# Expert tiles of a two-layer mixture-of-experts kernel: one transpose block on TensorE, the activation product ahead of the weight copies on VectorE, and empty scatter rows left out

## The chip, the cores and the metric

The kernel runs on one core of a Trainium2 chip. The metric is the device time of one launch in microseconds (us). A core has TensorE (PE in the rows; its weight loads have their own lines, PEld), VectorE (DVE), ScalarE (ACT), GpSimd (POOL) and SyncE (SP), each with its own instruction stream in program order, and 16 DMA engines that all queues share. SPq, POOLq and ACTq are the instructions of those engines that start a DMA.

## The reference

Two layers work on 256 latent tokens and 256 context tokens with 1024 channels. Each layer is a token mixer (state space, gated MLP, differential attention) followed by a mixture of experts: 64 experts of hidden width 256, eight of them chosen for each token, and one shared expert. The change touches the routed experts only:

```python
def swiglu(x, wg, wu, wd):
    return (jax.nn.silu(x @ wg) * (x @ wu)) @ wd

def routed_experts(h, eidx, w, w_gate, w_up, w_down):
    ...   # sort the (token, expert) pairs by expert, pad each expert's list to whole blocks
    def block_ffn(args):
        tok, wt, e = args
        return swiglu(h_pad[tok], w_gate[e], w_up[e], w_down[e]) * wt[:, None]
    yb = lax.map(block_ffn, (row_tok.reshape(n_blk, MOE_BLOCK), row_w.reshape(n_blk, MOE_BLOCK), blk_e))
    return jax.ops.segment_sum(yb.reshape(n_rows, d), row_tok, num_segments=t + 1)[:t]
```

Layer 0 routes 512 tokens (4096 pairs), layer 1 only the 256 latent ones (2048 pairs).

## The kernel before

Everything is float32. In each layer the mixer is followed by `route` (which tokens go to which unit of which expert), `experts` and `combine`.

**Units and tiles.** A unit is up to 64 tokens of one expert, a tile is two units (lanes) side by side on the 128 rows. The number of tiles follows from the data: 43 in layer 0 and 25 in layer 1, 68 in all. Rows of a unit that no token fills are empty. Tables in memory, made by `route`, say for each tile which token a row gathers (`t_gather`, an empty row's index lies out of bounds) and which row of `acc` it adds to (`t_scatter`, an empty row goes to one of 64 spare rows behind each lane's n rows).

**Weights.** A unit needs its expert's gate, up and down matrices, 3 MB in all. `load` (three DMAs from SP's queue) brings them into one of four slots of a ring `raw`; two tiles fill the ring. If the slot already holds that expert, the DMAs are skipped by a condition. From the slot DVE copies them on: gate and up in four pieces b = 0 to 3 for each lane (`copy_gu`, tiles `gu`, single-buffered across tiles), down in one piece for each lane (`copies_dn`, tiles `dn`, double-buffered). DVE waits for a unit's load with a semaphore that SP raises, and needs a register load (`TENSOR_LOAD`) for the slot's address and the count to wait for. When a lane's down copy is done the slot is free, and SP issues the load of the unit four further on; SP raises the signal for an earlier load only when it has issued later ones.

**A tile on TensorE.** `gate_up(t)` is 32 matmuls of 64-column weights, two at a time for the two lanes (`tile_position`), into `pg`. `x_t(t+1)` transposes the next tile's gathered rows, eight 128x128 transposes into `px`. `down(t-1)` is 16 matmuls of 64-column weights into `py`. `h_t(t-1)` transposes the activation `sg` of the earlier tile, two 128x128 transposes into `ph`. ACT does silu, the copies of `px` to `xt` and `ph` to `ht`, and scales `py` to `y`; DVE multiplies silu by up (`act`, L1580) and makes the weights of the rows (L1569); POOL issues the gather of three tiles ahead and the scatter of `y`, an indirect DMA that adds into `acc`.

**What sets the order.** `experts` is written under a manual schedule: each engine runs its instructions as the Python code emits them. `body(t)` emits h_t(t-1), gate_up(t), the gate/up copies of pieces 0 to 2 of tile t+1 (each lane after its own register load and wait), act(t), the copies of piece 3, x_t(t+1), the gather, down(t-1), and the down copies of tile t+1 with SP's loads. Tiles whose number depends on the data run under nested `If`s (`rest`); the last branch emits h_t and down of the last tile.

Of the kernel before, what the change touches and what calls it, by code (L numbers as in the profile page):

```python
# [11 lines left out]
F32 = mybir.dt.float32  # L12
# [3 lines left out]
ALU = mybir.AluOpType  # L16
AX = mybir.AxisListType
ET = mybir.EngineType
# [3 lines left out]
P = 128  # L22
D = 1024
# [4 lines left out]
T = NLAT + NCTX  # L28
# [32 lines left out]
def shape_consts():  # L61
# [7 lines left out]
    for n in (T, NLAT):  # L69
        pm, ln = p % UNIT, p // UNIT  # L70
        cols += [1 + n + pm, ln * (n + UNIT) + n + pm]
    for t in range(NT):
# [28 lines left out]
class Build:  # L101
# [1108 lines left out]
    def load(self, l, raw, eid, cond, slot_off):  # L1210
# [4 lines left out]
        for j, nm in enumerate(("w_exp_gate", "w_exp_up", "w_exp_down")):  # L1215
            w = self.A[nm][l][ds(e, 1)]
            src = w.rearrange("o (p k) n -> p (o k) n", p=P) if j < 2 else w.rearrange("o (k p) n -> p (o k) n", p=P)
            o = 2048 * j
# [22 lines left out]
    def route(self, l, n, rt, fD, acc, tab, raw, pool, pp):  # L1241
# [14 lines left out]
        nc.gpsimd.memset(zt, 0.0)  # L1256
        r0, r1 = n, LANES * (n + UNIT)
        while r0 < r1:
            m = min(P, r1 - r0)
            nc.scalar.dma_start(acc[r0:r0 + m, :], zt[:m])  # L1260
            r0 += m
        M = pool.tile([P, nt, NE], F32, name="M")
# [213 lines left out]
        pcc = self.C("pcol")  # L1476
        k1 = 1 if n == T else 3
        v = pool.tile([P, nx], F32, name="lv")
# [5 lines left out]
        V.tensor_copy(tb["gather"], g)  # L1484
        V.tensor_scalar(g, v, 0.5, None, op0=ALU.is_gt)
        V.tensor_scalar(g, g, pcc[:, k1:k1 + 1], -1.0, op0=ALU.mult, op1=ALU.mult)
        V.tensor_scalar(g, g, pcc[:, k1 + 1:k1 + 2], None, op0=ALU.add)
        V.tensor_add(g, g, v)
        tb["scatter"] = tab.tile([P, nx], I32, name="t_scatter")
# [3 lines left out]
    def experts(self, l, n, tb, fD, acc, raw):  # L1493
# [9 lines left out]
        with tc.tile_pool(name="ex", bufs=1, reuse_waits="tile") as pool, \  # L1503
# [5 lines left out]
            SG = [pool.tile([P, EH], F32, name="sg%d" % i) for i in range(2)]  # L1509
            HT = pool.tile([P, 2, P], F32, name="ht")  # L1510
            Y = [pool.tile([P, D], F32, name="y%d" % i) for i in range(2)]
# [16 lines left out]
            def copies_gu(t):  # L1528

                srcs = []  # L1530
                for ln in range(LANES):
                    u = t * LANES + ln
                    off, wv = regs(tb["unit"][0:1, 0:2, u], ET.DVE)
                    off = nc.s_assert_within(off, 0, (SLOTS - 1) * EW, skip_runtime_bounds_check_because=why)
                    V.wait_ge(s_ld, wv)
                    src = raw[:, ds(off, EW)]
                    srcs.append(src)
                    for b in range(3):
                        copy_gu(ln, b, src)
                return srcs  # L1540
# [41 lines left out]
            def h_t(t):  # L1582
                for k in range(2):
                    nc.tensor.transpose(pH[:, k * P:(k + 1) * P], SG[t % 2][:, k * P:(k + 1) * P], ident)
                nc.scalar.copy(HT.rearrange("p a b -> p (a b)"), pH[:, 0:256])  # L1585

            def down(t):
                for hf in range(2):
                    for k in range(2):
                        for ln in range(LANES):  # L1590
                            r = slice(UNIT * ln, UNIT * ln + UNIT)
                            nc.tensor.matmul(pY[hf][r, :], HT[:, k, r], DN[ln][t % 2][:, k, 512 * hf:512 * hf + 512],  # L1592
                                             start=(k == 0), stop=(k == 1), tile_position=(0, UNIT * ln))
                    nc.scalar.activation(Y[t % 2][:, 512 * hf:512 * hf + 512], pY[hf], AF.Copy, scale=W[t % 4])  # L1594
                nc.gpsimd.indirect_dma_start(out=acc, out_offset=bass.IndirectOffsetOnAxis(ap=tb["scatter"][:, t:t + 1], axis=0),  # L1595
                                             in_=Y[t % 2], in_offset=None, compute_op=ALU.add)

            def body(t):
                if t > 0:
                    h_t(t - 1)  # L1600
                gate_up(t)
                if t + 1 < tmax:
                    srcs = copies_gu(t + 1)
                act(t)
                if t + 1 < tmax:
                    for ln in range(LANES):
                        copy_gu(ln, 3, srcs[ln])
                    x_t(t + 1)
                if t + AHEAD < tmax:
                    gather(t + AHEAD)  # L1610
                if t > 0:
                    down(t - 1)
                if t + 1 < tmax:
                    copies_dn(t + 1, srcs)

            def rest(t):

                if t < tmax:
# [3 lines left out]
                    with more.Else():  # L1622
                        h_t(t - 1)
                        down(t - 1)
                else:
                    h_t(t - 1)
                    down(t - 1)
            for t in range(AHEAD):
                gather(t)
            srcs = copies_gu(0)  # L1630
            for ln in range(LANES):
                copy_gu(ln, 3, srcs[ln])
            copies_dn(0, srcs)
# [49 lines left out]
    def whole(self):  # L1683
# [8 lines left out]
        for l in range(DEPTH):  # L1692
# [3 lines left out]
            fD = self.dram.tile([n, D + NE], F32, name="f_%d" % l)  # L1696
            acc = self.dram.tile([LANES * (n + UNIT), D], F32, name="acc%d" % l)
            f = rows(fD, n // P)
# [37 lines left out]
```

## Time and profile before

| | |
|---|---|
| three runs | 2009.74, 2008.34 and 2000.35 us, median 2008.34 |
| the profiled execution | 2000.67 us, span 1998.8 us |
| mean granted TensorE clock | 0.941 |
| PE busy | 1792.3 us, 90% of the span |
| DVE, ACT, POOL busy | 1176.3, 595.6, 528.3 us |
| moved by DMA | 440.11 MB, 220 GB/s on the mean |
| expert tiles, layer 0 | about 634 to 1180 us, 43 tiles |
| expert tiles, layer 1 | about 1618 to 1966 us, 25 tiles |

A row of a timeline gives the start in us, the length in us, engine, line and operation, then what it writes and reads, how many like it follow one another, and in brackets how long the engine stood idle before and what released it. A row of the windows gives, for a stretch of time, the busy time of each engine with its number of instructions, then the granted clock, the share of time in which the DMA engines were busy, and the rate. A row of waits gives engine, line, what it waited for, the sum, the number and the longest.

### The profile page before, as it was taken

The page shows a single profiled execution, that of the slowest core. Times are in us where ns is not written, and L with a number is a line of the kernel's source. Part 1 is how long each engine was busy: PE and PEld are TensorE (multiplying, and loading weights), DVE is VectorE, ACT ScalarE, POOL GpSimd, SP SyncE. Part 2 cuts the span into 40 slices and gives each one's busy share as a digit, 9 for nine tenths or more (in the row PEclk, how much of TensorE's full clock was granted, in tenths as well). Part 3 has the DMA queues.
Part 4 walks back from the last instruction along what each step waited for, and adds up shares of the span by engine and source line. Part 5 has one row for each costly group of instructions (what it writes and reads, how often), then busy time and mean ns, then how long its engine had stood idle before and what let it go on. Part 6 is the DMA issues. An engine that isn't in the chain of part 4 may idle for free. (4 is left out here: it accounts for less than half of the span.)

```text
span 1998.8 us, 30455 instructions
## 1 busy us (share of the span) xinstructions
PE 1792.3 (90%) x10137; PEld 1040.6 (52%) x10137; DVE 1176.3 (59%) x2346; ACT 595.6 (30%) x1139; POOL 528.3 (26%) x407
## 2 busy tenths in 40 slices
PE   5798999999998999999998974989989689998894
PEld 2686876778765333333333323767789443333331
DVE  7687554333666666666665637823563666646563
ACT  3343343332222222222222215423453212221211
POOL 4354301222311222222222224321143012232221
PEclk8898999999999999999999976979999799999986
DMA  8113524453778677787898957346544379999974
GB/s 276 49 44 115 176 95 140 150 193 130 269 248 314 198 214 210 228 292 232 301 323 293 381 168 263 119 156 214 194 145 169 142 299 309 317 304 388 377 259 116
DMA packets 168310, 440.11 MB, mean 220 GB/s; under 512 B 26261, under 2 KB 82995, under 8 KB 151226
## 3 DMA queue, kind: packets, MB, share of 16 engines
q1 hardware_dynamic: 132044, 340.89, 46.6%
q0 software_dynamic: 20448, 62.41, 13.7%
q10 hardware_dynamic: 15630, 34.56, 4.8%
q8 instruction: 86, 1.41, 0.3%
q14 instruction: 102, 0.84, 0.1%
HBM read 658.36 MB, written 58.17 MB: 358 GB/s over the span
## 5 line engine op out<-in xcount | busy, mean ns | idle before, releaser
L1575 PE MATMUL pg<-gu,xt 128*64 128x512 f32 x2176 | 497.4, 610 | 1.5 <-ACT xt L1567 1.5
L1544 DVE COPY gu<-raw 128x1024 f32 x560 | 364.1, 694 | 207.8 <-SPq L1237 97.0
L1575 PEld LDWEIGHTS pg<-gu,xt 128*64 128x64 f32 x2176 | 153.8, 140 | 298.0 <-issue 283.7
L1595 POOL DMA_INDIRECT acc<-y,t_scatter x68 | 124.3, 1828 | 606.6 <-ACT ht L1585 430.0
L1592 PE MATMUL py<-dn,ht 128*64 128x512 f32 x1088 | 251.3, 604 | 5.4 <-ACT ht L1585 5.4
L1550 DVE COPY dn<-raw 128x2048 f32 x140 | 172.0, 1229 | 120.0 <-PE py L1592 100.5
L135 PE MATMUL mm<-uh,whi 128*128 128x512 f32 (+1 forms) x544 | 198.6, 365 | 6.8 <-ACT rx L848 4.6
L137 PE MATMUL mm<-uh,wlo 128*128 128x512 f32 (+1 forms) x544 | 194.9, 359 | 0.5 <-DVE wlo L314 0.5
L136 PE MATMUL mm<-ul,whi 128*128 128x512 f32 (+1 forms) x544 | 193.7, 356 | 0.0
L314 DVE TENSOR_TENSOR wlo<-raw,whi 128x1024 fp32r<-128x1024 f32 x77 | 97.8, 1271 | 114.1 <-ACT whi L311 113.9
L1579 ACT ACTIVATE sg<-pg 128x256 f32<-128x256 f32 x68 | 26.1, 384 | 452.1 <-PE pg L1575 452.1
L1524 POOL DMA_INDIRECT xg<-f,t_gather x74 | 101.0, 1365 | 180.8 <-DMA acc<-sh_y 56.2
L1592 PEld LDWEIGHTS py<-dn,ht 128*64 128x64 f32 x1088 | 72.8, 138 | 132.5 <-issue 118.7
L1594 ACT ACTIVATE y<-py,w 128x512 f32<-128x512 f32 x136 | 93.5, 687 | 161.2 <-PE py L1592 161.2
L311 ACT CAST whi<-raw 128x1024 fp32r<-128x1024 f32 x92 | 96.0, 1047 | 146.3 <-PE mm L136 117.7
L135 PEld LDWEIGHTS mm<-uh,whi 128*128 128x128 f32 x544 | 106.1, 195 | 31.7 <-issue 6.4
L137 PEld LDWEIGHTS mm<-uh,wlo 128*128 128x128 f32 x544 | 105.7, 194 | 18.5 <-issue 4.5
L136 PEld LDWEIGHTS mm<-ul,whi 128*128 128x128 f32 x544 | 106.0, 195 | 17.1 <-issue 4.5
L1566 PEld LDWEIGHTS px<-ct,xg 128*128 128x128 f32 x560 | 67.9, 194 | 57.4 <-issue 55.7
L1566 PE MATMUL px<-ct,xg 128*128 128x128 f32 x560 | 81.0, 288 | 0.9 <-DMA xg<-f,t_gather 0.9
L1567 ACT COPY xt<-px 128x512 f32<-128x512 f32 x140 | 75.3, 590 | 18.9 <-PE px L1566 17.9
L145 POOL TENSOR_TENSOR rs_r<-rs_ve,eps 128x1 f32<-128x1 f32 (+1 forms) x38 | 31.1, 822 | 178.5 <-DVE rs_ve L143 150.9
(473 smaller groups left out, 2738.8 us busy)
## 6 DMA issues: line engine op xcount, KB each, us to landing
raw<-in_w_exp_gate_dram SPq DMA_DIRECT2D x148, 1024.0 KB
raw<-in_w_exp_up_dram SPq DMA_DIRECT2D x148, 1024.0 KB
raw<-in_w_exp_down_dram SPq DMA_DIRECT2D x148, 1024.0 KB
raw<-in_w_in_dram SPq DMA_DIRECT2D x42, 1024.0 KB
mraw<-in_w_mod_dram SPq DMA_DIRECT2D x80, 512.0 KB
fraw<-in_w_mod_dram SPq DMA_DIRECT2D x16, 512.0 KB
cb_y<-acc SPq DMA_DIRECT2D x12, 512.0 KB
pj<-in_w_proj_da_dram SPq DMA_DIRECT2D x8, 512.0 KB
```

The source lines that it names most:

```text
L135: nc.tensor.matmul(out, lh, rh, start=start, stop=False)
L136: nc.tensor.matmul(out, lh, rl, start=False, stop=False)
L137: self.last = nc.tensor.matmul(out, ll, rh, start=False, stop=stop).ins
L311: self.nc.scalar.copy(hv, src)
L314: i = eng.tensor_tensor(lv, src, hv.bitcast(F32), op=ALU.subtract)
L1524: nc.gpsimd.indirect_dma_start(out=XG[t % AHEAD], out_offset=None, in_=fD, in_offset=bass.IndirectOffsetOnAxis(ap=tb["gather"][:, t:t + 1] ...
L1544: c = V.tensor_copy(GU[ln][b], gu[:, 2 * b:2 * b + 2])
L1550: c = V.tensor_copy(DN[ln][t % 2].rearrange("p a b -> p (a b)"), srcs[ln][:, 4096:6144])
L1566: nc.tensor.transpose(pX[hf][:, k * P:(k + 1) * P], XG[t % AHEAD][:, 4 * hf + k:D:8], ident)
L1575: nc.tensor.matmul(pG[t % 2][r, :], XT[t % 2][:, k, r], GU[ln][k // 2][:, k % 2].rearrange("p g n -> p (g n)"), start=(k == 0), stop=(k == ...
L1592: nc.tensor.matmul(pY[hf][r, :], HT[:, k, r], DN[ln][t % 2][:, k, 512 * hf:512 * hf + 512], start=(k == 0), stop=(k == 1), tile_position=( ...
L1595: nc.gpsimd.indirect_dma_start(out=acc, out_offset=bass.IndirectOffsetOnAxis(ap=tb["scatter"][:, t:t + 1], axis=0), in_=Y[t % 2], in_offse ...
```

## The change

- `body(t)` emits gate_up(t), act(t), x_t(t+1), all gate/up copies of tile t+1, h_t(t), the gather, down(t-1), and the down copies. The activation of tile t is transposed in its own iteration, right behind the row transposes; `ht` is double-buffered for that, and the last branch emits only down.
- `copies_gu` loads the registers of both lanes first, then copies piece 0 of lane 0 and of lane 1, then pieces 1, 2 and 3 with the lanes in turn. DVE's product stands ahead of all of it.
- The scatter gets a bound: an index beyond the last row of `acc` is left out. `acc` loses its spare rows, the zero fill gets fewer DMAs, and `route` makes the scatter index with three DVE operations fewer (the out-of-bounds index of an empty row is kept).
- The down matrix is loaded with two adjacent rows of it on a partition (one run of 8 KB rather than two of 4 KB); `h_t` reads every second column of `sg` to match.

```diff
@@ load
-            src = w.rearrange("o (p k) n -> p (o k) n", p=P) if j < 2 else w.rearrange("o (k p) n -> p (o k) n", p=P)
+            src = w.rearrange("o (p k) n -> p (o k) n", p=P)
@@ route
-        r0, r1 = n, LANES * (n + UNIT)
-        while r0 < r1:
-            m = min(P, r1 - r0)
-            nc.scalar.dma_start(acc[r0:r0 + m, :], zt[:m])
-            r0 += m
+        for r0 in range(n, LANES * n, P):
+            nc.scalar.dma_start(acc[r0:r0 + P, :], zt)
...
-        V.tensor_scalar(g, v, 0.5, None, op0=ALU.is_gt)
-        V.tensor_scalar(g, g, pcc[:, k1:k1 + 1], -1.0, op0=ALU.mult, op1=ALU.mult)
-        V.tensor_scalar(g, g, pcc[:, k1 + 1:k1 + 2], None, op0=ALU.add)
-        V.tensor_add(g, g, v)
+        V.tensor_scalar_add(g, g, pcc[:, k1:k1 + 1])
@@ experts
-            HT = pool.tile([P, 2, P], F32, name="ht")
+            HT = [pool.tile([P, 2, P], F32, name="ht%d" % i) for i in range(2)]
...
+                v = [regs(tb["unit"][0:1, 0:2, t * LANES + ln], ET.DVE) for ln in range(LANES)]
                 srcs = []
-                for ln in range(LANES):
-                    u = t * LANES + ln
-                    off, wv = regs(tb["unit"][0:1, 0:2, u], ET.DVE)
+                for ln, (off, wv) in enumerate(v):
                     off = nc.s_assert_within(off, 0, (SLOTS - 1) * EW, skip_runtime_bounds_check_because=why)
+                    srcs.append(raw[:, ds(off, EW)])
                     V.wait_ge(s_ld, wv)
-                    src = raw[:, ds(off, EW)]
-                    srcs.append(src)
-                    for b in range(3):
-                        copy_gu(ln, b, src)
+                    copy_gu(ln, 0, srcs[ln])
+                for b in range(1, 4):
+                    for ln in range(LANES):
+                        copy_gu(ln, b, srcs[ln])
                 return srcs
...
-                    nc.tensor.transpose(pH[:, k * P:(k + 1) * P], SG[t % 2][:, k * P:(k + 1) * P], ident)
+                    nc.tensor.transpose(pH[:, k * P:(k + 1) * P], SG[t % 2][:, k::2], ident)
...
-                                             in_=Y[t % 2], in_offset=None, compute_op=ALU.add)
+                                             in_=Y[t % 2], in_offset=None, bounds_check=LANES * n - 1, oob_is_err=False, compute_op=ALU.add)

             def body(t):
-                if t > 0:
-                    h_t(t - 1)
                 gate_up(t)
-                if t + 1 < tmax:
-                    srcs = copies_gu(t + 1)
                 act(t)
                 if t + 1 < tmax:
-                    for ln in range(LANES):
-                        copy_gu(ln, 3, srcs[ln])
                     x_t(t + 1)
+                    srcs = copies_gu(t + 1)
+                h_t(t)
                 if t + AHEAD < tmax:
                     gather(t + AHEAD)
                 if t > 0:
                     down(t - 1)
@@ rest
-                        h_t(t - 1)
                         down(t - 1)
...
-            acc = self.dram.tile([LANES * (n + UNIT), D], F32, name="acc%d" % l)
+            acc = self.dram.tile([LANES * n, D], F32, name="acc%d" % l)
```

On TensorE, from the end of a tile's gate/up matmuls to the start of the next tile's, in layer 0 (`px` row transposes, `py` down, `ph` activation transposes, `pg` gate/up), before:

```order
L1575 MATMUL pg_5963<-gu_3_5946,xt_5938 64x512
L1566 MATMUL px_5960<-ct,xg_5395 128x128 x4
L1566 MATMUL px_5961<-ct,xg_5395 128x128 x4
L1592 MATMUL py_5965<-dn_0_5947,ht 64x512
...
L1592 MATMUL py_5966<-dn_0_5949,ht 64x512
L1584 MATMUL ph<-ct,sg_5952 128x128 x2
L1575 MATMUL pg_5962<-gu_0_5939,xt_5937 64x512
```

and after:

```order
L1569 MATMUL pg_5960<-gu_3_5942,xt_5934 64x512
L1560 MATMUL px_5957<-ct,xg_5395 128x128 x4
L1560 MATMUL px_5958<-ct,xg_5395 128x128 x4
L1578 MATMUL ph<-ct,sg_5948 128x128 x2
L1586 MATMUL py_5962<-dn_0_5943,ht_5949 64x512
...
L1586 MATMUL py_5963<-dn_0_5945,ht_5949 64x512
L1569 MATMUL pg_5959<-gu_0_5935,xt_5933 64x512
```

The two activation transposes now follow the eight row transposes, and belong to the tile whose gate/up has just ended; the down matmuls stand next to the following tile's gate/up matmuls.

On VectorE in the same iteration, one tile's copies and product (lane 0 writes the `gu` tiles 5939 to 5942, lane 1 5943 to 5946), before:

```order
L1207 TENSOR_LOAD t_unit
...
L1544 COPY gu_0_5939<-raw 128x1024
...
L1207 TENSOR_LOAD t_unit
...
L1544 COPY gu_0_5943<-raw 128x1024
...
L1544 COPY gu_2_5945<-raw 128x1024
L1580 TENSOR_TENSOR sg_5951<-sg_5951,pg_5962 128x256
...
L1544 COPY gu_3_5942<-raw 128x1024
...
L1544 COPY gu_3_5946<-raw 128x1024
```

and after:

```order
L1574 TENSOR_TENSOR sg_5947<-sg_5947,pg_5959 128x256
L1563 SCALAR_TENSOR_TENSOR xg_5394,w_5954<-ct_62,t_eid,xg_5394 128x64
L1206 TENSOR_LOAD t_unit x2
...
L1538 COPY gu_0_5935<-raw 128x1024
...
L1538 COPY gu_0_5939<-raw 128x1024
...
L1538 COPY gu_3_5942<-raw 128x1024
...
L1544 COPY dn_1_5944<-raw 128x2048
```

The product and the row weights stand ahead of both register loads and of the waits for the next tile's weights; the eight copies follow with the lanes in turn, and the down copies come behind the eighth.

## Rows read from the trace of the kernel before

**Rows 1.** The windows view, four stretches of the two expert stages:

```profile
658.10:1080.20 422.10, 422.10 (x2031) 155.39 (x2030) 283.72 (x456) 108.50 (x211) 108.06 (x70) 1.00 0.80 257
1080.20:1157.90 77.70, 63.36 (x291) 22.91 (x290) 39.71 (x63) 16.18 (x31) 17.72 (x11) 0.93 0.96 340
1618.20:1784.30 166.10, 157.10 (x738) 57.58 (x738) 104.75 (x170) 40.75 (x77) 40.05 (x25) 0.98 0.87 301
1784.30:1944.60 160.30, 141.11 (x640) 50.71 (x638) 90.50 (x148) 34.23 (x66) 38.22 (x22) 0.93 0.95 350
```

**Rows 2.** Timeline of one undisturbed tile of layer 0, parts of it:

```profile
766.66 7.09 PE L1575 MATMUL pg<-gu,xt 128*64 128x512 f32 x32
...
768.96 0.34 SPq L1225 DMA_DIRECT2D raw<-in_w_exp_gate_dram  x1
...
773.67 0.97 PEld L1566 LDWEIGHTS px<-ct,xg 128*128 128x128 f32 x8 [0.81 <-issue]
773.68 1.16 PE L1566 MATMUL px<-ct,xg 128*128 128x128 f32 x8
...
773.79 0.38 ACT L1579 ACTIVATE sg<-pg 128x256 f32<-128x256 f32 x1 [6.41 <-PE pg L1575]
...
774.64 0.41 DVE L1580 TENSOR_TENSOR sg<-sg,pg 128x256 f32<-128x256 f32 x1
...
774.77 3.65 PE L1592 MATMUL py<-dn,ht 128*64 128x512 f32 x16
...
775.25 0.14 PEld L1592 LDWEIGHTS py<-dn,ht 128*64 128x64 f32 x2 [0.28 <-issue]
...
778.35 0.20 PEld L1584 LDWEIGHTS ph<-ct,sg 128*128 128x128 f32 x2 [0.81 <-issue]
...
778.45 1.23 DVE L1550 COPY dn<-raw 128x2048 f32 x1 [1.99 <-PE py L1592]
...
778.72 1.51 PE L1575 MATMUL pg<-gu,xt 128*64 128x512 f32 x6
```

**Rows 3.** Waits in layer 0's expert stage, 629 to 1185 us:

```profile
DVE gu L1544 <- SPq L1237: 29.9, 8, 10.6
...
PE ph L1584 <- DVE sg L1580: 16.3, 4, 8.4
```

**Rows 4.** The same view of layer 1's expert stage, 1617 to 1975 us:

```profile
DVE gu L1544 <- SPq L1237: 67.1, 18, 10.1
...
PE ph L1584 <- DVE sg L1580: 28.2, 10, 6.0
```

**Rows 5.** Timeline, a wait for weights in each layer:

```profile
1098.06 1.90 DVE L1544 COPY gu<-raw 128x1024 f32 x3 [10.59 <-SPq L1237]
...
1100.96 1.12 PE L1575 MATMUL pg<-gu,xt 128*64 128x512 f32 x2
...
1798.03 3.70 DVE L1544 COPY gu<-raw 128x1024 f32 x6 [10.05 <-SPq L1237]
...
1802.74 1.12 PE L1575 MATMUL pg<-gu,xt 128*64 128x512 f32 x2
```

**Rows 6.** Timeline, the first tiles of layer 1 and the last of layer 0:

```profile
1627.46 3.85 DVE L1544 COPY gu<-raw 128x1024 f32 x6 [0.53 <-DVE xg L1569]
...
1631.69 0.69 PE L1584 MATMUL ph<-ct,sg 128*128 128x128 f32 x2 [4.81 <-DVE sg L1580]
...
1174.23 5.21 PE L1592 MATMUL py<-dn,ht 128*64 128x512 f32 x16 [2.68 <-ACT ht L1585]
```

**Rows 7.** The page's DMA queues, packets, MB, share: the indirect one:

```profile
q0 software_dynamic: 20448, 62.41, 13.7%
```

**Rows 8.** DMA view of 1783 to 1930 us: packets, MB, share of 16 engines:

```profile
q1 hardware_dynamic: 8284, 46.75, 78.0%
q0 software_dynamic: 2885, 8.29, 23.4%
```

**Rows 9.** DMA view of 1186 to 1200 us, where rows of 4 KB are read:

```profile
q1 hardware_dynamic: 1513, 5.54, 99.9%
```

More of the change, by code (lines that the diff above doesn't have):

```diff
@@ L69, in shape_consts @@
     for n in (T, NLAT):
-        pm, ln = p % UNIT, p // UNIT
-        cols += [1 + n + pm, ln * (n + UNIT) + n + pm]
+        cols.append(p // UNIT * n)
     for t in range(NT):
@@ L1476, in route @@
         pcc = self.C("pcol")
-        k1 = 1 if n == T else 3
+        k1 = 1 if n == T else 2
         v = pool.tile([P, nx], F32, name="lv")
@@ L1583, in h_t @@
                 for k in range(2):
-                    nc.tensor.transpose(pH[:, k * P:(k + 1) * P], SG[t % 2][:, k * P:(k + 1) * P], ident)
-                nc.scalar.copy(HT.rearrange("p a b -> p (a b)"), pH[:, 0:256])
+                    nc.tensor.transpose(pH[:, k * P:(k + 1) * P], SG[t % 2][:, k::2], ident)
+                nc.scalar.copy(HT[t % 2].rearrange("p a b -> p (a b)"), pH[:, 0:256])
             def down(t):
@@ L1591, in down @@
                             r = slice(UNIT * ln, UNIT * ln + UNIT)
-                            nc.tensor.matmul(pY[hf][r, :], HT[:, k, r], DN[ln][t % 2][:, k, 512 * hf:512 * hf + 512],
+                            nc.tensor.matmul(pY[hf][r, :], HT[t % 2][:, k, r], DN[ln][t % 2][:, k, 512 * hf:512 * hf + 512],
                                              start=(k == 0), stop=(k == 1), tile_position=(0, UNIT * ln))
@@ L1622, in rest @@
                     with more.Else():
-                        h_t(t - 1)
                         down(t - 1)
                 else:
-                    h_t(t - 1)
                     down(t - 1)
@@ L1630, in experts @@
             srcs = copies_gu(0)
-            for ln in range(LANES):
-                copy_gu(ln, 3, srcs[ln])
             copies_dn(0, srcs)
```

## The prediction

> **What bounds the kernel now.** I read the windows view first, by stretches of the two expert stages, because the change touches little else. [rows 1] shows two regimes. From 658.10 to 1080.20 us TensorE is busy for all of 422.10 us at clock 1.00, 35 tiles of 12.06 us: there the bound is TensorE's own sequence. In the other three stretches TensorE is idle for a part, the clock is below 1.00, and the DMA engines are busy for 0.87 to 0.96 of the time. Against 12.06 us a tile the excess is 77.70 - 5 x 12.06 = 17.4 us (tiles 37 to 41 of layer 0), 166.10 - 13 x 12.06 = 9.3 us (the first 13 tiles of layer 1) and 160.30 - 11 x 12.06 = 27.6 us (its next 11). The waits say whose fault that is: VectorE waits for loads of weights 8 times in layer 0 [rows 3] and 18 times in layer 1 [rows 4], and TensorE for VectorE's product 4 and 10 times. The product is queued behind the copies that wait for the load, so one late load stops h_t and then gate_up.
>
> **TensorE's sequence.** From the starts in [rows 2] a tile is gate_up 7.02 us (766.66 to 773.68), x_t 1.09, down 3.58, h_t 0.37, together 12.06. Sixteen pairs of gate_up against eight pairs of down differ by 3.44 us, 0.43 a pair, so each block carries 7.02 - 16 x 0.43 = 0.14 us on top; eight transposes against two differ by 0.72 us, 0.12 each, and 0.13 is on top again. After the change x_t and h_t are one block, and down and the next gate_up are another: two blocks for four, 2 x 0.135 = 0.27 us a tile less. The lower bound is half of that, if only one side of a switch costs; a loss is in the rivals. I take 0.27, since both differences of the rows give the same price. It counts where TensorE is the bound: the 35 tiles, and about 12 others that wait for nothing: 47 x 0.27 = 12.7 us (6 to 13).
>
> The weight loads show a gap of 0.81 us at both changes from 64 to 128 columns, 0.28 inside a block [rows 2]; one of the two goes, and if the difference were all time of TensorE's, that would be 0.53 us a tile, 25 us rather than 12.7. The starts of the matmuls do not bear out so much. The Trainium skill ("TensorEngine Tiling (Array Packing)", section "Tiling Modes") says that changing the tiling mode, not just the tile, drains TensorE. By that rule four drains a tile become two; the 0.27 us above is what the trace gives for two, and 12.7 us the sum by it.
>
> **Does h_t(t) wait for its product?** It now comes right behind x_t(t+1). In [rows 2] gate_up ends at 773.75, silu starts 0.04 later and takes 0.38, the product takes 0.41; with like handoffs of 0.05 it is done at 774.68, and x_t ends at 774.77. The margin is 0.09 us, and it holds only while VectorE is free at that moment. VectorE is: copies can start at about E + 2.0 (E is the end of gate_up; product, row weights and two register loads come first, each some 0.53 as in the gap ahead of 1627.46 [rows 6]), eight take 8 x 0.63 (the six at 1798.03 took 3.70) and the two down copies 1.23 each with 0.24 between them, so it is done at about E + 9.95 of 11.8 us. I take nothing for it; 0.3 us a tile would cost all of the 12.7 again.
>
> **Does gate_up(t+1) wait for its copies?** Its first pieces of both lanes are there at E + 2.0 + 1.3 = E + 3.3, and it is due at E + 4.7; later pieces follow every 1.3 us against 1.75 us that gate_up takes over a piece. This costs nothing if the load is there by E + 2, and a load may come about 1.4 us later than that without harm.
>
> **Waits for weights.** In [rows 5] one lane's load comes at 1098.06, and gate_up starts 2.90 us later: three copies, product, h_t. At 1798.03 six copies stand before it, 4.71 us. After the change only the first piece of the waited lane (0.63) or of both (1.3) does, so gate_up would start 2.2 or 3.4 us sooner after the signal. But against that stands the slot: the down copies, which free it, move from behind two copies to behind eight. In [rows 2] the first of them starts at 778.45, and ends at E + 5.9; after, E + 8.45. So SP, which issues the next load 1.3 us after the copy (768.96 against 778.45 + 1.23 - 12.06 = 767.62), does so 2.5 us later, and everything queued behind that wait on SP, the signal for an earlier load too. After a stall, where the copies start late in both kernels, the difference is about 1 us. Where the DMA engines have no gap, a later issue costs nothing, because the transfer would only stand in the queue.
>
> For tiles 37 to 41, some three waits that TensorE sees, at 2.2 less 1.0 give 3.6, and the empty rows (below) a little: 4 us (0 to 8). In layer 1 the first wait is of another kind: six copies and the product stand between 1627.46 and h_t, a wait of 4.81 us [rows 6]; with two copies it shrinks by 3.4 us. The start of layer 0 has the same order of copies but a part of them comes earlier; between 0 and 3.4 I take 1 us. For the rest of the 9.3 us in that stretch I take half, 3 us (0 to 5).
>
> **Empty scatter rows.** Rows gathered are (512 + 256) x 8 = 6144, of 68 x 128 = 8704. If the gather moves only valid rows (1088 floats, 4352 B) and the scatter all, the queue should carry 26.74 + 35.65 = 62.39 MB; it carries 62.41 [rows 7]. So an out-of-bounds index moves no bytes, and 2560 rows of 4 KB, 10.5 MB, go from the scatters. The queue's time is 13.7% of 1998.8 us for 62.41 MB, 4.4 us of all 16 engines a MB: 46 us, but only where DMA is the bound is it time. In layer 1's second half [rows 8] the price is 0.234 x 147 / 8.29 = 4.15 us a MB, and 11 tiles x 46 empty rows x 4 KB are 2.08 MB: 8.6 us. There q1 and q0 together take 101% of the engines, so I take it in full, with 3 us for the last wait of the stretch: 11.6 us (3 to 20; a row that adds reads and writes and may be dearer than the mean).
>
> **Edits near nothing.** Longer runs for down: a MB of 4 KB rows took 0.999 x 14 x 16 / 5.54 = 40.4 us of one engine [rows 9], q1's mix 0.780 x 147 x 16 / 46.75 = 39.2 [rows 8]. If only 4 KB runs are dearer, 8 KB ones cost 38.6, and the stretch would gain 1.8 us; I take 0 (0 to 2). Strided columns in h_t: x_t reads every eighth column already, at 0.12 us a transpose. Three VectorE operations and two zero fills in `route`: none stands in a wait seen here; 0 to 1 us a layer. The tail: down waited 2.68 us for `ht` [rows 6] and will not, but SP's last conditional loads, which come before the combine's reads on the same queue, move back by as much: 0 (0 to 6).
>
> **The sum.** 12.7 + 4 + 3.4 + 1 + 3 + 11.6 = 35.7 us off the profiled execution's 2000.67 us: 1965. That execution is the fastest but one of four; the median of the three runs is 2008.34, and off it the sum gives about 1972 us, which I forecast.
>
> **The rivals.** *The slot decides (slower).* If the DMA engines run dry between the end of a load and the next issue, the 2.5 us reach every just-in-time load. Of 26 waits, each 2.5 us longer, that is 65 us, against 12.7 + 4 + 3.4 + 1 + 3 = 24 us that the order gives and 11.6 of the scatters, which no longer bound: 2008 + 65 - 24 = 2049 us at worst; it is slower at all from 24 / 26 = 0.9 us a wait, and by over 10 us from 1.3. Against it speak the shares of 0.95 and 0.96 in the stretches where the waits are [rows 1]; for it, that 0.80 in the first stretch leaves room for new waits. *Gains cancel (no change).* h_t waits 0.3 us for the product in every tile (-12.7) and the slot takes back what the earlier start gives in layer 1 and tiles 37 to 41; the start and a part of the scatters remain: about 12 us, 1997. *Empty rows still cost their share (faster, less).* An index left out may keep most of its price in descriptors; then 27 us remain, 1981. *The switch is dearer*, 0.53 us a tile: 1960.
>
> **Chances.** The forecast with its bounds 0.60, dearer switch 0.10, empty rows still priced 0.12, gains cancel 0.10, slot decides 0.08. What a measurement of this kernel can tell from no change is about 0.5%, 10 us: faster is below 1998, slower above 2018. Part of the cancelling case lies below 1998 and part of the forecast's bounds above it: faster 0.80, same 0.13, slower 0.07. The range, 1945 to 2002, takes in the dearer switch with an upper bound or two (scatters at 20, tail at 6) and the cancelling case.
>
> **What would show it.** Undisturbed tiles of about 11.8 us; TensorE waiting for the product almost nowhere, and for `gu` copies instead, in fewer and shorter waits; q0 at about 51.9 MB; the second half of layer 1 about 12 us shorter with the DMA share still above 0.9. I am wrong if tiles keep 12.06 us (h_t waits for the product, or a merged block saves nothing), if VectorE's waits for loads grow in sum beyond 97 us, or if the DMA share in layer 1 falls while the tiles take as long.

## The result

The changed kernel takes 1974.74 us in the median of four runs (1971.67 to 1983.37), the kernel before 2004.34 (four runs, 1990.9 to 2009.74): a ratio of 0.988, 95% interval 0.9838 to 0.9922. In a second set of runs (`after_again`, six against eleven) it was 1967.8 against 2006.38, ratio 0.982, interval 0.9768 to 0.9871. The forecast was 1972 us, 1945 to 2002, faster.

The profiled execution is the slowest of its four, 1983.37 us with a span of 1981.6. It reached the first gate_up of layer 0 at 646.4 us, 12.5 us later than the profiled execution of before. That is no effect of the change: a second trace of the same changed kernel (`after_again`) got there at 633.6, its variants between 634.6 and 643.2, and the kernel before at 633.8 and 641.8.

The page of after, the busy lines and the indirect queue (packets, MB, share of 16 engines; before in [rows 7]):

```profile
PE 1786.6 (90%) x10137; PEld 1064.9 (54%) x10137; DVE 1162.7 (59%) x2340; ACT 594.9 (30%) x1139; POOL 566.7 (29%) x407
...
q0 software_dynamic: 20448, 51.95, 11.2%
```

The windows view of after, the same four groups of tiles as in [rows 1] (tiles 2 to 36 and 37 to 41 of layer 0, tiles 43 to 55 and 56 to 66 in layer 1):

```profile
668.90:1085.10 416.20, 416.20 (x2032) 162.05 (x2030) 276.31 (x456) 108.98 (x210) 138.74 (x70) 1.00 0.76 251
1085.10:1148.00 62.90, 60.58 (x293) 23.48 (x290) 37.42 (x62) 15.54 (x30) 16.84 (x10) 1.00 1.01 386
1617.90:1775.50 157.60, 153.34 (x740) 61.55 (x742) 103.68 (x173) 40.16 (x77) 43.99 (x24) 1.00 0.84 298
1775.50:1925.50 150.00, 139.39 (x642) 52.93 (x640) 88.09 (x145) 34.19 (x66) 38.41 (x22) 0.95 0.95 360
```

In the first group TensorE is busy throughout in both kernels: 35 tiles take 416.2 us, 11.89 us each, where they took 12.06. The other three groups got 14.8, 8.5 and 10.3 us shorter, at a DMA share of 1.01, 0.84 and 0.95 where it was 0.96, 0.87 and 0.95: about as busy, for less time, with the same weights and fewer scattered rows.

The waits of after in layer 0's expert stage, 620 to 1180 us:

```profile
DVE gu L1538 <- SPq L1236: 13.5, 5, 6.4
PE pg L1569 <- DVE gu L1538: 7.6, 3, 3.8
```

and in layer 1's, 1600 to 1975 us:

```profile
DVE gu L1538 <- SPq L1236: 29.5, 11, 7.8
...
PE pg L1569 <- DVE gu L1538: 14.5, 5, 5.2
```

VectorE's waits for loads fell from 97 us [rows 3, 4] to 43. TensorE no longer waits for the product behind the copies; its waits are for the copies themselves, 22 us against 44.5. The second traces show less of a fall: 65.5 to 38.4 us for VectorE, 35.3 to 16.2 for TensorE. Since these waits differ from one execution to the next, here are two traces of each kernel, with two experiments that are told next. The columns are the times between the starts of the gate_up of tiles 2, 37, 42 (layer 0) and 43, 56, 67 (layer 1):

| kernel | 35 tiles | 5 tiles | 13 tiles | 11 tiles | sum | time, ratio to before (95%) |
|---|---|---|---|---|---|---|
| before | 422.1 | 77.7 | 166.1 | 160.3 | 826.2 | |
| before_again | 422.1 | 70.4 | 162.3 | 158.1 | 812.9 | |
| rows_only | 422.2 | 66.9 | 159.7 | 150.7 | 799.5 | 1986.56, 0.9892 (0.9852 to 0.9931) |
| order_only | 416.3 | 68.9 | 162.3 | 156.7 | 804.2 | 1984.27, 0.9898 (0.9831 to 0.9966) |
| after | 416.3 | 62.8 | 157.6 | 150.0 | 786.7 | 1974.74, 0.988 (0.9838 to 0.9922) |
| after_again | 416.3 | 65.2 | 153.0 | 146.8 | 781.3 | 1967.8, 0.982 (0.9768 to 0.9871) |

The means of before and after differ by 819.6 - 784.0 = 35.6 us. The first two tiles of layer 0 add 2.6 (24.3 and 27.5 us before, 22.5 and 24.2 after).

### The profile page after: what moved, and what is told of

It is laid out like the page before. It is cut to its first block, busy times and chain, and to the rows that moved or that the text cites. A ratio compares the mean times of both kernels' runs of the same rounds, so it can differ in the third digit from the quotient of the medians.

```text
span 1981.6 us, 30632 instructions
## 1 busy us (share of the span) xinstructions
PE 1786.6 (90%) x10137; PEld 1064.9 (54%) x10137; DVE 1162.7 (59%) x2340; ACT 594.9 (30%) x1139; POOL 566.7 (29%) x407
## 2 busy tenths in 40 slices
DMA packets 159830, 428.60 MB, mean 216 GB/s; under 512 B 28789, under 2 KB 85523, under 8 KB 134554
## 3 DMA queue, kind: packets, MB, share of 16 engines
q0 software_dynamic: 20448, 51.95, 11.2%
## 5 line engine op out<-in xcount | busy, mean ns | idle before, releaser
L1538 DVE COPY gu<-raw 128x1024 f32 x560 | 345.6, 689 | 95.6 <-SPq L1236 42.9
L1589 POOL DMA_INDIRECT acc<-y,t_scatter x68 | 184.2, 2709 | 570.7 <-DVE gu L1538 325.8
L1569 PEld LDWEIGHTS pg<-gu,xt 128*64 128x64 f32 x2176 | 162.4, 139 | 343.3 <-issue 263.7
L1574 DVE TENSOR_TENSOR sg<-sg,pg 128x256 f32<-128x256 f32 x68 | 28.7, 421 | 191.6 <-ACT sg L1573 191.6
L1518 POOL DMA_INDIRECT xg<-f,t_gather x74 | 79.0, 1067 | 157.7 <-DVE t_scatter L1484 65.4
```

What stands on the lines that cost most here:

```text
L1518: nc.gpsimd.indirect_dma_start(out=XG[t % AHEAD], out_offset=None, in_=fD, in_offset=bass.IndirectOffsetOnAxis(ap=tb["gather"][:, t:t + 1] ...
L1538: c = V.tensor_copy(GU[ln][b], gu[:, 2 * b:2 * b + 2])
L1569: nc.tensor.matmul(pG[t % 2][r, :], XT[t % 2][:, k, r], GU[ln][k // 2][:, k % 2].rearrange("p g n -> p (g n)"), start=(k == 0), stop=(k == ...
```

## The experiments

**The two halves of the change apart.** `order_only` is the changed kernel with the scatter of before; the 8 KB runs for down and the columns of `h_t` stay as changed (the diff leaves out the zero fills and constants that go with it):

```diff
...
-                                             in_=Y[t % 2], in_offset=None, bounds_check=LANES * n - 1, oob_is_err=False, compute_op=ALU.add)
+                                             in_=Y[t % 2], in_offset=None, compute_op=ALU.add)
...
+        V.tensor_scalar(g, v, 0.5, None, op0=ALU.is_gt)
+        V.tensor_scalar(g, g, pcc[:, k1:k1 + 1], -1.0, op0=ALU.mult, op1=ALU.mult)
...
-            acc = self.dram.tile([LANES * n, D], F32, name="acc%d" % l)
+            acc = self.dram.tile([LANES * (n + UNIT), D], F32, name="acc%d" % l)
```

> The changed kernel with the empty rows put back (spare rows of acc, the three index operations, no bound on the scatter); the order on the engines, the double-buffered ht and the 8 KB runs for down stay. Theory: the expert stages (first gate_up to last) lost 35 us in the traces, 68 x 0.17 = 11.6 of them as the shorter tile, the rest as shorter waits; the order alone keeps the 0.17 us a tile and the shorter starts, and gives back what the scatters cost where DMA is the bound, some 12 us: expert stages about 23 us below before, time about 1982. Rival, rows do nearly all of the waits' part: stages about 13 us below before, time about 1992. Rival, rows do nothing: as the changed kernel, about 1975.

`rows_only` makes the opposite edit to the kernel before (the same lines, plus and minus exchanged).

> The kernel before with only the empty rows left out of the scatter (bound, index, fewer spare rows and zero fills). Theory: undisturbed tiles keep 12.06 us, q0 carries 51.95 MB, and the waits for weights shrink by about 12 us in sum, nearly all in layer 1: time about 1992. Rival, rows do nearly all of the waits' part: about 24 us less, 1980. Rival, rows do nothing: 2004. The bounded scatter holds GpSimd longer (2.7 against 1.8 us in the mean); if that delays gathers, tiles show waits for them.

The sums in the table: rows alone 819.6 - 799.5 = 20 us, rows on top of the order 804.2 - 784.0 = 20 us; order alone 819.6 - 804.2 = 15.4 us, order on top of the rows 799.5 - 784.0 = 15.5 us. The two add up. The order was expected to bring more and the rows less: the skipped rows are the larger part. Both are faster than before by about 1%, and their intervals overlap, so the split rests on the traces, one execution each, where the same kernel's sums differ by 5 to 13 us. That the two add up speaks for it, and so do the later runs: seven traces with both parts (after, `after_again`, `plain_columns`, `sorted_silu`, `slot_late_own`, `slot_early` and `combined`) lie between 781.2 and 786.7, clear of either part alone. The windows view of the last eleven tiles, `order_only` and then `rows_only`:

```profile
1772.50:1929.50 157.00, 143.15 (x642) 56.33 (x640) 89.82 (x146) 34.21 (x66) 39.60 (x22) 0.93 0.97 357
```

```profile
1780.20:1930.90 150.70, 138.65 (x639) 50.16 (x638) 89.74 (x144) 34.41 (x67) 35.26 (x22) 0.95 0.95 351
```

With a DMA share of 0.97 and 0.95 the order alone gains 2.5 us on the mean of before (159.2), the rows alone 8.5.

**TensorE's place for the transposes alone.** `dve_only_order` puts h_t back ahead of the next gate_up:

```diff
             def body(t):
+                if t > 0:
+                    h_t(t - 1)
                 gate_up(t)
...
-                h_t(t)
...
```

> The changed kernel with the two activation transposes put back to where they stood, ahead of the next gate_up, behind down; VectorE's order (product first, lanes in turn) and the left-out rows stay. Theory: TensorE has its four blocks again, so undisturbed tiles take 12.06 us; the waits are as short as in the changed kernel, since it is VectorE's order that shortens them: expert stages 68 x 0.17 = 11.6 us longer than in the changed kernel, time about 1986. Rival, the transposes' place shortens the waits too: over 15 us longer.

Measured: 1984.12 us, ratio 0.9915 (0.9877 to 0.9953). Its groups take 424.7, 63.1, 161.0 and 148.4 us, 13 more than after: 8.4 in the 35 tiles where TensorE is the bound, 5.7 in the thirteen of layer 1 (against the mean of the two traces of after), none in the other two. So the shorter waits come with VectorE's order and the rows, and the shorter tile with the transposes' place. But the tile takes 12.13 us here, not 12.06. The timeline shows where, in h_t and the gate_up behind it (the first two rows are x_t and down):

```profile
775.22 1.16 PE L1560 MATMUL px<-ct,xg 128*128 128x128 f32 x8
...
776.32 3.65 PE L1586 MATMUL py<-dn,ht 128*64 128x512 f32 x16
...
779.90 0.51 PE L1578 MATMUL ph<-ct,sg 128*128 128x128 f32 x2
...
780.34 4.08 PE L1569 MATMUL pg<-gu,xt 128*64 128x512 f32 x18
```

h_t takes 0.44 us from start to start, where it took 0.37 in [rows 2], in the same place. What differs in h_t is that it reads every second column of `sg`.

**What h_t costs in its new place.** One tile of after (timeline):

```profile
770.98 0.97 PEld L1560 LDWEIGHTS px<-ct,xg 128*128 128x128 f32 x8 [0.81 <-issue]
770.98 1.16 PE L1560 MATMUL px<-ct,xg 128*128 128x128 f32 x8
771.09 0.38 ACT L1573 ACTIVATE sg<-pg 128x256 f32<-128x256 f32 x1 [6.09 <-PE pg L1569]
771.51 0.42 DVE L1574 TENSOR_TENSOR sg<-sg,pg 128x256 f32<-128x256 f32 x1 [3.06 <-ACT sg L1573]
...
771.99 0.50 PE L1578 MATMUL ph<-ct,sg 128*128 128x128 f32 x2
...
772.42 0.20 PEld L1586 LDWEIGHTS py<-dn,ht 128*64 128x64 f32 x4
772.42 3.65 PE L1586 MATMUL py<-dn,ht 128*64 128x512 f32 x16
...
775.90 7.04 PE L1569 MATMUL pg<-gu,xt 128*64 128x512 f32 x32
...
777.17 3.27 POOL L1589 DMA_INDIRECT acc<-y,t_scatter  x1 [7.26 <-DVE gu L1538]
...
777.64 1.22 DVE L1544 COPY dn<-raw 128x2048 f32 x1
...
779.10 1.23 DVE L1544 COPY dn<-raw 128x2048 f32 x1 [0.24 <-DVE dn L1544]
```

x_t takes 1.01 us, h_t 0.43, down 3.48, gate_up 6.97 (775.90 to 782.87). The product ends at 771.93 and h_t starts at 771.99. Between down and gate_up the gap of the weight loads is gone. `no_product_wait` lets h_t transpose old data (the down matmuls then work on other numbers, and as layer 1 routes by them it has 23 tiles there; only the length of a tile is compared):

```diff
-                    nc.tensor.transpose(pH[:, k * P:(k + 1) * P], SG[t % 2][:, k::2], ident)
+                    nc.tensor.transpose(pH[:, k * P:(k + 1) * P], XT[t % 2][:, k, :], ident)
```

> The changed kernel with h_t transposing two pieces of xt, long written, instead of the fresh product (so the down matmuls work on other numbers); nothing else moves. Theory: a merged block saves 0.135 us at each of two places, but h_t waits about 0.10 us in each tile for the product, so that tiles take 11.89 and not 11.79 us; here they take 11.79, and the expert stages lose some 4 us more where TensorE is the bound. Rival, no wait, the merged block itself saves less: tiles stay at 11.89 us.

Tiles took 11.76 us (1950.16 us in all, with fewer tiles). The timeline of one:

```profile
769.78 1.16 PE L1560 MATMUL px<-ct,xg 128*128 128x128 f32 x8
...
770.77 0.38 PE L1578 MATMUL ph<-ct,xt 128*128 128x128 f32 x2
771.08 3.65 PE L1586 MATMUL py<-dn,ht 128*64 128x512 f32 x16
774.57 7.04 PE L1569 MATMUL pg<-gu,xt 128*64 128x512 f32 x32
...
781.53 0.71 PE L1560 MATMUL px<-ct,xg 128*128 128x128 f32 x4
```

x_t 0.99, h_t 0.31, down 3.49, gate_up 6.96. So the two merged blocks are worth 12.06 - 11.76 = 0.30 us, and 0.13 of that is lost again in after, nearly all in h_t (0.43 against 0.31). This edit took away two things at once, the fresh product and the stride. Two runs part them. `plain_columns` loads down as before and reads adjacent columns:

```diff
-            src = w.rearrange("o (p k) n -> p (o k) n", p=P)
+            src = w.rearrange("o (p k) n -> p (o k) n", p=P) if j < 2 else w.rearrange("o (k p) n -> p (o k) n", p=P)
...
-                    nc.tensor.transpose(pH[:, k * P:(k + 1) * P], SG[t % 2][:, k::2], ident)
+                    nc.tensor.transpose(pH[:, k * P:(k + 1) * P], SG[t % 2][:, k * P:(k + 1) * P], ident)
```

> The changed kernel with down's weights loaded in two runs of 4 KB again and the activation transposed from adjacent columns. In dve_only_order h_t took 0.44 us (779.90 to 780.34) where before it took 0.37; in no_product_wait a tile took 11.76. Theory: reading every second column costs 0.07 us in h_t, and the wait for the product the remaining 0.06: here tiles take 11.82 us, 5 us less over 68 tiles, and the packets of 4 KB cost nothing: time about 1966. Rival, the wait for the product is all 0.13: tiles stay at 11.89. Rival, 4 KB runs cost: DMA-bound tiles lose what the others gain.

`sorted_silu` keeps the load and has silu write the columns sorted:

```diff
-                nc.scalar.activation(SG[t % 2], pG[t % 2][:, 0:EH], AF.Silu)
-                V.tensor_mul(SG[t % 2], SG[t % 2], pG[t % 2][:, EH:2 * EH])
+                sg = SG[t % 2].rearrange("p (k j) -> p k j", k=2)
+                nc.scalar.activation(sg, pG[t % 2][:, 0:EH].rearrange("p (j k) -> p k j", k=2), AF.Silu)
+                V.tensor_mul(sg, sg, pG[t % 2][:, EH:2 * EH].rearrange("p (j k) -> p k j", k=2))
```

> The changed kernel, 8 KB runs kept, with silu writing its columns sorted (even ones, then odd ones) and the product reading up's columns in the same order, so that h_t reads adjacent columns. Theory, if the stride costs in h_t: tiles of 11.82 us if sorted columns cost ScalarE and VectorE nothing; if silu or the product get longer by more than 0.07, that comes back as a wait of h_t and tiles take 11.89 or more. Time 1966 to 1971.

Both have tiles of 11.83 us. The timeline of one in `sorted_silu`, x_t, h_t, down and the next gate_up:

```profile
778.94 1.16 PE L1560 MATMUL px<-ct,xg 128*128 128x128 f32 x8
...
779.95 0.44 PE L1579 MATMUL ph<-ct,sg 128*128 128x128 f32 x2
780.32 3.65 PE L1587 MATMUL py<-dn,ht 128*64 128x512 f32 x16
...
783.80 1.03 PE L1569 MATMUL pg<-gu,xt 128*64 128x512 f32 x4
```

h_t is back at 0.37, so the stride costs 0.06 us a tile, and the remaining 0.07 to 11.76 goes with reading the fresh product; silu and the product stay at 0.38 and 0.42 us with sorted columns. In time the two are 1968.57 (0.9849, 0.9774 to 0.9924) and 1969.92 us (0.9855, 0.9778 to 0.9931), not to be told from after. `plain_columns`, which moves down in 4 KB runs, takes 783.7 us over the four groups, `sorted_silu` 781.7, between or near the two traces of after (786.7, 781.3): no cost of the shorter runs shows.

**The slot.** The rival was that the slots, freed 2.5 us later, decide. In undisturbed tiles they come free 1.9 us later: with E the end of gate_up, the two down copies end at E + 5.93 and E + 7.40 before, and at E + 7.83 and E + 9.30 after. `slot_late` frees them 1.23 us later still, by a second copy:

```diff
             def copies_dn(t, srcs):
+                V.tensor_copy(DN[0][t % 2].rearrange("p a b -> p (a b)"), srcs[0][:, 4096:6144])
                 for ln in range(LANES):
```

> The changed kernel with lane 0's down copy done twice, so that both slots of a tile come free 1.23 us later (VectorE is then done at about E + 11.2 of 11.89 us, E the end of gate_up). Theory: where weights are late the DMA engines have no gap, so a later issue costs little: under 5 us in all, and nothing in undisturbed tiles. Rival, the slot decides: each of some 16 waits for loads 1.2 us longer, 15 to 20 us.

It took 2287.2 us, ratio 1.14. Its waits view (640 to 1300 us) tells why:

```profile
DVE dn L1543 <- DMA raw<-in_w_exp_down_dram: 197.9, 15, 17.9
```

The added copy did not carry the ring's own semaphore, so it waited for every load in flight into `raw`. That measures a wait that no kernel here has, and nothing of the slot. `slot_late_own` ties the copy to its own load:

```diff
+                own(V.tensor_copy(DN[0][t % 2].rearrange("p a b -> p (a b)"), srcs[0][:, 4096:6144]), "r", "w")
```

> The slots freed 1.23 us later once more, by a second copy of lane 0's down weights, which this time is tied to its own load alone; in slot_late the second copy waited for every load in flight into the ring, up to 17.9 us, so that run told nothing of the slot. Theory: the waits for weights come from DMA that has no gap, not from the slot: excess over equal tiles in the two expert stages within 5 us of the changed kernel's 20 to 24, undisturbed tiles 11.89, time about 1970 to 1978. Rival, the slot decides: 15 to 20 us more excess, about 1988.

Measured: 1974.37 us, ratio 0.988 (0.9805 to 0.9954); the groups take 416.3, 64.1, 158.0 and 147.6 us, 786.0 in sum, as after. `slot_early` frees the slots sooner (`dve_regs` makes the register loads that stood in `copies_gu`):

```diff
...
             def body(t):
+                v = dve_regs(t + 1) if t + 1 < tmax else None
                 gate_up(t)
...
-                for b in range(1, 4):
-                    for ln in range(LANES):
-                        copy_gu(ln, b, srcs[ln])
+                for b, ln in ((1, 0), (1, 1), (2, 0), (3, 0)):
+                    copy_gu(ln, b, srcs[ln])
...
             def copies_dn(t, srcs):
                 for ln in range(LANES):
+                    if ln:
+                        copy_gu(1, 2, srcs[1])
+                        copy_gu(1, 3, srcs[1])
```

> The changed kernel with VectorE's register loads done in the idle time ahead of the product, and lane 0's pieces and down copy finished ahead of lane 1's last two pieces: slots free about 2.5 us (lane 0) and 1.0 us (lane 1) sooner. Theory: as DMA has no gap where the waits are, at most 5 us faster. Rival, the slot decides: 15 to 30 us faster. Lane 1's last pieces come at E + 7.3, and gate_up needs the third at about E + 8.4: if that is too late, undisturbed tiles get longer than 11.89 us.

Measured: 1973.0 us, ratio 0.9847 (0.9779 to 0.9915); 416.3, 63.0, 156.7 and 147.3 us, 783.3 in sum. It lost some 4 us in the first two tiles (27.8 us), where lane 1's last pieces stood behind a down copy that waited. The product and the two down copies of an undisturbed tile:

```profile
779.94 0.42 DVE L1578 TENSOR_TENSOR sg<-sg,pg 128x256 f32<-128x256 f32 x1 [3.39 <-ACT sg L1577]
...
784.54 1.23 DVE L1548 COPY dn<-raw 128x2048 f32 x1 [0.35 <-PE py L1590]
...
787.23 1.21 DVE L1548 COPY dn<-raw 128x2048 f32 x1
```

They end 5.83 and 8.50 us behind the start of the product, where they end 7.35 and 8.82 behind it in after (771.51 to 778.86 and 780.33): the slots came free 1.5 us (lane 0) and 0.3 us (lane 1) sooner, less than the 2.5 and 1.0 that were expected. Slots 1.2 us later, or sooner by these amounts, leave the waits in the tiles as they are.

What the later slot does cost shows at the end of layer 0: the last of the conditional loads that the last tile issues, and the combine's first addition to what it read of `acc`, with the start of the last x_t ahead; before:

```profile
1166.11 1.16 PE L1566 MATMUL px<-ct,xg 128*128 128x128 f32 x8
...
1178.39 0.08 SPq L1225 DMA_DIRECT2D raw<-in_w_exp_down_dram  x1
...
1192.46 2.34 POOL L1673 TENSOR_TENSOR cb_y<-cb_y,cb_y 128x1024 f32<-128x1024 f32 x1 [9.93 <-DMA cb_y<-acc]
```

after:

```profile
1162.70 1.16 PE L1560 MATMUL px<-ct,xg 128*128 128x128 f32 x8
...
1176.51 0.08 SPq L1224 DMA_DIRECT2D raw<-in_w_exp_down_dram  x1
...
1191.17 2.34 POOL L1659 TENSOR_TENSOR cb_y<-cb_y,cb_y 128x1024 f32<-128x1024 f32 x1 [10.71 <-DMA cb_y<-acc]
```

and `slot_early`:

```profile
1155.99 1.16 PE L1564 MATMUL px<-ct,xg 128*128 128x128 f32 x8
...
1168.28 0.08 SPq L1224 DMA_DIRECT2D raw<-in_w_exp_down_dram  x1
...
1182.54 2.34 POOL L1664 TENSOR_TENSOR cb_y<-cb_y,cb_y 128x1024 f32<-128x1024 f32 x1 [10.32 <-DMA cb_y<-acc]
```

The addition starts 26.4 us after the last x_t in before, 28.5 in after, 26.6 in `slot_early`; the last load is issued at 12.3, 13.8 and 12.3 us. The change pays about 2 us there. The other traces agree: 26.9 us in `before_again`, 26.6 in `combined`, which has the copies of `slot_early`, and 28.5 to 30.0 in the other runs with the new order. At the end of layer 1 the same interval is 27.8 and 30.0 us in the two traces of before and 29.9 and 29.1 in those of after, so no cost can be told there.

**Repeats, and both remedies together.** The second traces of the changed kernel and of before are in the table.

> The changed kernel once more, for a second trace and more times. Its profiled execution took 12.5 us longer than that of before up to the first gate_up of layer 0, though the instructions up to there are nearly the same. If that belonged to the one execution, this trace starts its first gate_up at about 634 to 640 us and the whole takes about 1973; if the change did it (the few instructions of the routing that stand in another order), it starts at about 646 again.

> The kernel before once more, for a second trace: how far the waits of its expert stages vary from one execution to another. The changed kernel's two traces had 24 and 21 us of excess over equal tiles; before had 55 in its one. Theory: 50 to 60 us again, tiles of 12.06. If it has under 35, the shortening of the waits is smaller than the traces suggested.

`after_again` reached its first gate_up at 633.6 us. `before_again` had less waiting than the first trace and than expected (812.9 us against 826.2, which is 41 us above 64 tiles of 12.06), so one trace alone would have overstated the gain in the five tiles of layer 0. `combined` joins `sorted_silu` and `slot_early`, with the first tile's copies as in after (the diff shows that last part, the rest stands above):

```diff
-            srcs = copies_gu(0, dve_regs(0))
-            copies_dn(0, srcs)
+            srcs = copies_gu(0, dve_regs(0), [(b, ln) for b in range(1, 4) for ln in range(LANES)])
+            copies_dn(0, srcs, ())
```

> sorted_silu and slot_early together, with the first tile's copies in the changed kernel's order. sorted_silu had tiles of 11.83 us; slot_early had the first read of acc by the combine 18.9 us after layer 0's last gate_up, against 20.4 to 20.8 in the changed kernel, but lost some 4 us in the first two tiles, where lane 1's last pieces stood behind a down copy that waited. Theory: 68 x 0.06 = 4 us and 2 us at the end of layer 0, each as in its own run, nothing lost in the first tiles: about 6 us below the changed kernel, 1962 to 1968. Rival: lane 1's third piece comes at E + 7.1 and gate_up is due there sooner by 0.06; tiles that wait for it are longer than 11.83.

Measured: 1968.46 us, ratio 0.9849 (0.9814 to 0.9885); tiles of 11.83 us, 782.5 in the four groups. The trace has the shorter tile, 23.4 us in the first two tiles and layer 0's first addition 26.6 us behind the last x_t, but no gain over after can be told in time: the changed kernel's own medians are 1974.74 and 1967.8.

## Why the prediction was right

The sum, 35.7 us, met 35.6 us in the four groups and 2.6 in the first tiles, less about 2 at the end of layer 0. But that is in part luck: it is a right sum of terms that erred both ways, with the empty rows worth nearly twice their term and the order's shorter waits about half of theirs.

- **The shorter tile.** Forecast 0.27 us, bounds 0.13 to 0.27; measured 0.17. The price of the blocks was slightly low (0.30 for two, by `no_product_wait`), 0.15 us for each of the two blocks that went, and not the 0.53 us of the weight loads' gap. The Trainium skill ("TensorEngine Tiling (Array Packing)", section "Tiling Modes") says that a change of tiling mode drains TensorE. The trace agrees in that fewer changes took less time; that the 0.15 us is a drain, no run here shows. That both differences of [rows 2] gave 0.13 to 0.14 was luck in part: x_t read every eighth column there and h_t adjacent ones, and the same working on `dve_only_order`, where h_t reads every second column (x_t 1.10 us, h_t 0.44), gives 0.11 a transpose and 0.22 on top. Two terms put at nothing took 0.13 back: the handoff of the product, where I counted a margin of 0.09 us and 0.07 are lost, and the stride, where I argued from x_t, which reads every eighth column at 0.12 us a transpose; h_t got 0.06 longer with every second column. That failed step was an argument by likeness where the row for it did not exist.
- **Empty rows.** Forecast 11.6 us, only in layer 1's second half; measured 20 by two comparisons. There the term was nearly right (8.5 by `rows_only`, against 8.6 for the rows themselves). What was missing is the other two groups with waits, at shares of 0.96 and 0.87: about 7 us in the five tiles and 4.5 in the thirteen by `rows_only` against the mean of before, 5 and 7 by after against `order_only`. I had read 0.96 in [rows 1] for the five tiles and still put their rows at a little. The price per MB was about right: q0's time fell from 13.7% of 1998.8 to 11.2% of 1981.6 us, 52 us of 16 engines for 10.46 MB, 5.0 us a MB against 4.4 and 4.15. Rows left out move no bytes, as read off the gather.
- **Waits by the order.** Forecast 4 + 3.4 + 1 + 3 = 11.4 us, besides 12.7 for the tile; the order as a whole brought 15.4 us (`order_only` against the mean of before), of which 64 x 0.17 = 10.9 us are the shorter tile if all of it counts. So it shortened the waits of the four groups by some 4.5 us, the five tiles' (5.2 us in all) above others, or 7 with the 2.6 of the first tiles. The five tiles' 4 us came, then. The step that failed is the 3.4 + 3 us for the first thirteen tiles of layer 1. Its start did go as forecast: from the first gate_up to the second it took 14.1 and 15.3 us in the two traces of before, 10.5 and 9.7 in those of after and 9.8 in `order_only`. But over the thirteen tiles `order_only` brought only 1.9 us against the mean of before, less than the 2.2 that 13 shorter tiles are worth, and on top of the rows the order brought 4.4, about 2 beyond the shorter tiles: so much of what the start gained was lost again later in the stretch. In the last eleven tiles the order alone brought 2.5 us. That an earlier start only moves the wait where DMA has no gap is argued, not shown: the five tiles had a share of 0.96 too, and gained.
- **The slot.** The rival was put at 0.08, with the argument that DMA has no gap. `slot_late_own` and `slot_early` bear out that the slot does not decide in the tiles, for shifts of 1.2 us later and 1.5 and 0.3 sooner; they do not test the reason. The shift itself is 1.9 us and not 2.5: the copies start and run a little sooner than E + 2.0 and 0.63 each, and the forecast's own terms add to E + 8.3 for the first down copy and E + 9.7 for the second, not 8.45 and 9.95. At the end of layer 0 the later loads were forecast to cancel the earlier down; they cost 2 us.
- **What the profile would show.** Tiles of about 11.8 us were 11.89, q0 at 51.9 MB is 51.95, TensorE's waits for the product are gone, the DMA share in the second half of layer 1 stayed at 0.95, and the second half of layer 1 is 10.8 us shorter in the means against 12.

The whole-time forecast scaled the sum from the median of three runs. The medians of before were 2000 to 2006 in five sets of runs, so the base alone moves such a forecast by some 6 us.

What stays open: the split of 20 and 15 us rests on single traces of `rows_only` and `order_only`, and within it the shares of the five and the thirteen tiles change with the comparison; and why the product's handoff costs 0.07 us when it ends about when x_t does was not tried further.

## What to carry to other kernels

Look at the DMA share of each stretch with waits before pricing an earlier start: in the last eleven tiles, at 0.95, an earlier start brought 2.5 us and fewer bytes 8.5. Price the bytes in every stretch with waits and a busy DMA, not only the longest; here the two that were left out were together worth more than the one counted. Merging blocks of the same tile shape on TensorE is worth a price that can be read off as block time less the matmuls' steady pace (0.30 us for two blocks here), but check what the merged step now waits for and how its operand lies. A copy that frees a buffer sets, besides the next load, whatever else stands behind it on the loading queue, here the reads at the end of a layer.

## What the runs showed of the hardware that I had not expected

Left-out rows still leave their packets: q0 has 20448 packets with and without them. Packets under 512 B in the whole program went from 26261 to 28789, 2528 more where 2560 rows were left out, so nearly all of them seem to remain as small ones.

The scatter held GpSimd for 2.7 us on the mean, against 1.8 before, and the bound has nothing to do with it. `rows_only`, with the bound:

```profile
L1588 POOL DMA_INDIRECT acc<-y,t_scatter x68 | 123.4, 1814 | 604.8 <-ACT ht L1578 498.8
```

`order_only`, without it:

```profile
L1596 POOL DMA_INDIRECT acc<-y,t_scatter x68 | 184.5, 2713 | 579.9 <-DVE gu L1545 356.5
```

What differs is the VectorE copies beside it. In the tile of after shown above the scatter starts at 777.17, runs beside the end of the gate/up copies and both down copies, and ends at 780.44, 0.11 us behind the second down copy. In the tile of before it starts later against these copies and ends 0.11 us behind the second one too:

```profile
767.40 1.80 POOL L1595 DMA_INDIRECT acc<-y,t_scatter  x1 [8.65 <-ACT ht L1585]
...
767.86 1.23 DVE L1550 COPY dn<-raw 128x2048 f32 x1 [0.24 <-DVE dn L1550]
```

So it is with most: in 51 of 68 scatters of before and 54 of after the end comes about 0.12 us behind the end of such a copy. In `slot_early`, where mostly gate/up copies stand beside it, it takes 1.79 us; at the end of a layer, with VectorE idle, 1.57 in both kernels. So the scatter seems to wait for VectorE's copies to end; no run here was made to show why. Nothing waited for it here.
